# Storing the prompt's keys, values, gate scratch and mixer outputs through GpSimd's DMA queue

## The chip, the cores and the metric

The kernel runs on one core of a Trainium2 chip. The metric is the device time of one execution in microseconds. Three runs of the kernel before took 1498.4, 1499.0 and 1500.19 us, the median is 1499.0.

A core has five engines, each with an instruction queue of its own that runs strictly in order: TensorE (PE), VectorE (DVE), ScalarE (ACT), GpSimd (POOL) and SyncE (SP), which only issues transfers. A transfer (DMA) is issued from an engine's queue and then moved by the core's 16 DMA engines. Issuing stops the queue until the data that the transfer reads is ready and its target is free.

## The reference

One layer of a hybrid decoder, for a prompt of 2048 rows and 64 sample rows. What is computed:

```python
h = rms_norm(x, g_norm); proj = h @ w_in            # 1024 -> 3584
u, va, za, q, k, vb, zb = split(proj)
# mixer A: 4 groups of 128 channels, chunks of 128 rows
a = rms_norm(u * (tril(w_s) @ rms_norm(va) + b_s)) * silu(za)
# mixer B: 8 heads of 64; q, k normalised; patterns (128,1), (512,4), (2048,16)
for (w, r) in PATTERNS:                             # query t sees t - j*r, j = 0..w//r
    o_i, lse_i = banded_softmax_attention(q, k, vb, w // r, r)
b = rms_norm(sum_i softmax_i(lse) * o_i) * silu(zb)
h = x + concat(a, b) @ w_out
y = h + sigmoid(h @ w_ple_gate) * rms_norm(p @ w_ple)
# outputs: y (prompt, sample), k and vb of the prompt, k, vb and va of the samples
```

The sample rows do the same against a cache of 2048 keys and values for each of 8 sequences.

## The kernel before

The input projection is done in eight column chunks, `order = A0, B0, B1, A1, B2, B3, A2, A3`: A chunks hold u, v, z of one gMLP group, B chunks q, k, v, z of two heads (a head pair). Each chunk goes over 16 tiles of 128 prompt rows and one of the 64 sample rows (`gemm`, L441), three accumulators in PSUM. After every four tiles (512 rows) a group is finished:

- `b_norm` (L496 and on) normalises q and k and writes to HBM: the keys `ko` and values `vo`, which are outputs, the values in half-precision halves `v16` (to `vscr`, read back by the attention's `vload`), and the gate `gz` (to `zscr`).
- `a_norm` and later `a_mix` (L605 and on) compute the gMLP group, in place in the tile `ua`, and store it into `catd` (L634), 512 columns wide for mixer A.

Attention (`attn`, `scores`, `stage_c`) runs in small units that a pump in the program slips between the matmuls of the next chunks. Each unit takes scores, splits the exponentials into two halves `pc` on VectorE, lets SyncE transpose them by DMA into `pT` (L712), and multiplies with the values. Each pattern's partial result `rec` goes to HBM (r1d, r2d, r3d).

When a head pair is through, `comb_load` (L815, L818) loads the three partial results (`rl`, three buffers in all) and the gate (`gzl`, one buffer) for 512 rows, and `combine` merges them: the subtractions and `rl` merges (L826 to L835), a square, a reciprocal root on GpSimd (L187), the product with the gate (L850), and the store into `catd` (L852). Four combinations follow one another for each head pair. Those of the last pair (B3) run while chunk A3 is projected; at the same time the weights of the output stage are loaded (`wprep3`, L864), squared for their scale (L873), and split into halves (L888, L889), and the sample rows' attention begins, in which GpSimd multiplies cache rows with queries (L1184).

The output stage (`p3_*`) reads `catd` rows, tile by tile, and makes y.

The buffers that matter: `vo` and `ko` share two (`tmpA`), `gz` has two, `ua` two (`raw`), `gzl` one. A buffer is free again when its store has landed.

The order on each engine's queue is not the program's: the framework lists the instructions by a model of their times (`schedule_with_timeline_sim=True`), so an edit in one place can move instructions on all engines behind it.

Of the kernel before, what the change touches and what calls it, by code (L numbers as in the profile page):

```python
# [21 lines left out]
P = 128  # L22
# [119 lines left out]
def tile_hymba_gmlp_dilated_attn_step(  # L142
# [6 lines left out]
    nc = tc.nc  # L149
# [10 lines left out]
    kwin = k_win.rearrange("l b s h d -> (l b s) (h d)")  # L160
    vwin = v_win.rearrange("l b s h d -> (l b s) (h d)")
# [15 lines left out]
    def nm(s):  # L177
        uid[0] += 1
        return f"{s}_{uid[0]}"


    def small(n, tag=None, bufs=4, p=P):
        return sml.tile([P, n], F32, name=nm("sm"), tag=tag or f"s{n}", bufs=bufs)

    def rsqrt(src, n, p=P):
        y = small(n, f"rsy{n}")[:p]
        nc.gpsimd.tensor_tensor(y, src, mhalf[:p, :n], op=ALU.pow)  # L187
        return y
# [50 lines left out]
    zscr = [drm.tile([T, P], F32, name=f"zscr{i}") for i in range(4)]  # L239
# [3 lines left out]
    catd = [drm.tile([512, D], F32, name=f"catd{i}") for i in range(4)]  # L243
# [252 lines left out]
    def b_norm(G, sc, gch):  # L496
        m, n, hp, jg = G["m"], G["n"], G["hp"], G["jg"]
        c0 = hp * P
        ms = small(16, "bms", 2)
        nc.vector.tensor_scalar(ms[:m, :4 * n], G["ss"][:m, :4 * n], 2.0 ** -24 / HD, sc[:m, 5:6], op0=ALU.mult, op1=ALU.add)  # L500
        y = rsqrt(ms[:m, :4 * n], 4 * n, m)
        y4 = y.rearrange("p (j a) -> p j a", a=4)
        kv = G["raw"][:m, :n, 128:256].rearrange("p j (h d) -> p j h d", d=HD)
        qv = G["raw"][:m, :n, 0:128].rearrange("p j (h d) -> p j h d", d=HD)
        if m == P:
            ko = wk.tile([P, 4, P], F32, name=nm("ko"), tag="tmpA", bufs=2)
            for q in range(n):
                for h in range(2):
                    nc.vector.scalar_tensor_tensor(qv[:, q, h], qv[:, q, h], y4[:, q, h:h + 1], gqk,
                                                   op0=ALU.mult, op1=ALU.mult)  # L510
                nc.vector.tensor_tensor(kv[:, q], kv[:, q], y4[:, q, 2:4].unsqueeze(2).to_broadcast([P, 2, HD]),
                                        op=ALU.mult)
                nc.vector.tensor_tensor(ko[:, q, :].rearrange("p (h d) -> p h d", d=HD), kv[:, q],
                                        gkS.unsqueeze(1).to_broadcast([P, 2, HD]), op=ALU.mult)
        else:
            for h in range(2):
                nc.vector.scalar_tensor_tensor(qv[:, 0, h], qv[:, 0, h], y4[:, 0, h:h + 1], gqS[:m],
                                               op0=ALU.mult, op1=ALU.mult)
                nc.vector.scalar_tensor_tensor(kv[:, 0, h], kv[:, 0, h], y4[:, 0, h + 2:h + 3], gkS[:m],
                                               op0=ALU.mult, op1=ALU.mult)  # L520
        gzv = G["gz"][:m, :n, :]
        nc.vector.tensor_tensor(gzv, gzv, gch[:m, 0, :].unsqueeze(1).to_broadcast([m, n, P]), op=ALU.mult)
        if m == P:
            r0 = jg * 512
            rows = lambda t, a, w: t[r0:r0 + 512, a:a + w].rearrange("(j p) c -> p j c", p=P)
            nc.sync.dma_start(rows(kwin, c0, P), ko)
            nc.sync.dma_start(rows(vwin, c0, P), G["vo"])
            nc.sync.dma_start(rows(vscr[hp], 0, 258), G["v16"])
            nc.sync.dma_start(rows(zscr[hp], 0, P), G["gz"])
        else:  # L530
            gs = G["gz"][:m, 0, :]
            nc.vector.tensor_scalar(gs, gs, sc[:m, 2:3], None, op0=ALU.mult)
            qo, ko, vo = G["raw"][:m, 0, 0:128], G["raw"][:m, 0, 128:256], G["vo"][:m, 0, :]
            nc.sync.dma_start(knew[:, c0:c0 + P], ko)
            nc.sync.dma_start(kd[:, c0:c0 + P], ko)
            nc.sync.dma_start(vnew[:, c0:c0 + P], vo)
            nc.sync.dma_start(vd[:, c0:c0 + P], vo)
            nc.sync.dma_start(qd[:, c0:c0 + P], qo)
            nc.sync.dma_start(gzd[:, c0:c0 + P], gs)
# [65 lines left out]
    def a_mix(G, sc, gch):  # L605
        m, n, g, jg = G["m"], G["n"], G["g"], G["jg"]
        c0 = g * P
        pm = pst("t", 1)
        if m == P:
            with behind():  # L610
                nc.tensor.matmul(pm, lhsT=wsT[:, g, 0, :], rhs=G["vh"], start=True, stop=False)
            nc.tensor.matmul(pm, lhsT=wsT[:, g, 0, :], rhs=G["vl"], start=False, stop=False)
            nc.tensor.matmul(pm, lhsT=wsT[:, g, 1, :], rhs=G["vh"], start=False, stop=True)
            bb, mul = bsT, cS
        else:
            with behind():
                nc.tensor.matmul(pm[:m, 0:P], lhsT=bd8[:, g, :], rhs=G["va"][:m, 0, :], start=True, stop=True)
            bb, mul = bsS, 1.0
        pv = pm[:m, :n * P].rearrange("p (j c) -> p j c", c=P)
        t = G["va"][:m, :n, :]  # L620
        nc.vector.scalar_tensor_tensor(t, pv, mul, gch[:m, 1, :].unsqueeze(1).to_broadcast([m, n, P]),
                                       op0=ALU.mult, op1=ALU.mult)
        nc.vector.scalar_tensor_tensor(t, t, bb[:m, g:g + 1], G["u"][:m, :n, :], op0=ALU.add, op1=ALU.mult)
        s2 = small(4, "as2", 2)
        for q in range(n):
            nc.scalar.activation(G["u"][:m, q, :], t[:, q, :], AF.Square, accum_out=s2[:m, q:q + 1])
        ms = small(4, "ams", 2)
        nc.vector.tensor_scalar(ms[:m, :n], s2[:m, :n], 1.0 / P, sc[:m, 3:4], op0=ALU.mult, op1=ALU.add)
        y = rsqrt(ms[:m, :n], n, m)
        nc.vector.tensor_scalar(y, y, sc[:m, 2:3], None, op0=ALU.mult)  # L630
        for q in range(n):
            nc.vector.scalar_tensor_tensor(t[:, q], t[:, q], y[:, q:q + 1], G["gz"][:m, q, :], op0=ALU.mult, op1=ALU.mult)
        if m == P:
            nc.sync.dma_start(catd[jg][:, c0:c0 + P].rearrange("(j p) c -> p j c", p=P), t)  # L634
        else:
            nc.sync.dma_start(cats[:, c0:c0 + P], t[:, 0, :])

# [183 lines left out]
    def combine(hp, jg, sc, rr, gz):  # L821
        e = small(24, "e24", 2).rearrange("p (i a) -> p i a", i=3)
        nb = [t[:, :, HD + 1] for t in rr]
        mn = small(8, "mn8", 2)
        nc.vector.tensor_tensor(mn, nb[0], nb[1], op=ALU.min)
        nc.vector.tensor_tensor(mn, mn, nb[2], op=ALU.min)  # L826
        for i in range(3):
            nc.vector.tensor_tensor(e[:, i, :], mn, nb[i], op=ALU.subtract)
        ef = e.rearrange("p i a -> p (i a)")
        nc.scalar.activation(ef, ef, AF.Exp)  # L830
        t0 = rr[0][:, :, 0:65]
        nc.vector.tensor_tensor(t0, t0, e[:, 0, :].unsqueeze(2).to_broadcast([P, 8, 65]), op=ALU.mult)
        for i in (1, 2):
            for a in range(8):
                nc.vector.scalar_tensor_tensor(t0[:, a], rr[i][:, a, 0:65], e[:, i, a:a + 1], t0[:, a],  # L835
                                               op0=ALU.mult, op1=ALU.add)
        o = rr[0][:, :, 0:64]
        sq = rr[1][:, :, 0:64]
        nc.scalar.activation(sq, o, AF.Square)
        ss = small(8, "css", 2)  # L840
        nc.vector.tensor_reduce(ss, sq, axis=AX.X, op=ALU.add)
        dn = small(8, "cdn", 2)
        nc.vector.tensor_tensor(dn, rr[0][:, :, 64], rr[0][:, :, 64], op=ALU.mult)
        nc.vector.tensor_scalar(dn, dn, sc[:, 4:5], None, op0=ALU.mult)
        nc.vector.scalar_tensor_tensor(dn, ss, 1.0 / HD, dn, op0=ALU.mult, op1=ALU.add)
        y = rsqrt(dn, 8)
        nc.vector.tensor_scalar(y, y, sc[:, 2:3], None, op0=ALU.mult)
        g8 = gz.rearrange("p j (h d) -> p (j h) d", h=2)
        for a in range(8):
            nc.vector.scalar_tensor_tensor(g8[:, a], o[:, a], y[:, a:a + 1], g8[:, a], op0=ALU.mult, op1=ALU.mult)  # L850
        c0 = 512 + hp * P
        nc.sync.dma_start(catd[jg][:, c0:c0 + P].rearrange("(j p) c -> p j c", p=P), gz)  # L852

    big = {}

# [475 lines left out]
    for ci, (kind, i) in enumerate(order):  # L1331
# [9 lines left out]
        G = None  # L1341
        for j in range(NT + 1):
# [25 lines left out]
            if j % 4 == 0 and j < NT:  # L1368
                G = (b_group if kind == "B" else a_group)(i, j // 4, 4, P)
# [120 lines left out]
```

## Time and profile before

| | |
|---|---|
| median of 3 runs | 1499.0 us |
| profiled execution | 1500.87 us |
| its span | 1499.2 us |
| TensorE busy | 1299.3 us, 87% |
| VectorE busy | 1059.2 us, 71% |
| ScalarE busy | 781.1 us, 52% |
| GpSimd busy | 313.9 us, 21% |
| DMA, SyncE's queue | 262.73 MB, 78.7% of 16 engines |
| DMA, GpSimd's queue | 1.66 MB, 0.7% of 16 engines |
| granted TensorE clock | 0.95 of full |

Busy time is a share of the whole span; it says little about a single stage, where another engine or a transfer may come last. The stages by time: weights and A0 up to some 125 us, projection with attention up to some 880, the combination of the last head pair with the loads of the output weights up to some 1020, then the output stage with the sample rows' attention. The 80 stores that the change touches lie between 82.3 and 1016.1 us.

### The profile page before, as it was taken

To read this page: it belongs to the slowest core of one execution; us is meant where nothing else is said; L and a number is where in the kernel's file an instruction comes from. 1 tells how busy PE (TensorE), PEld (TensorE's weight loads), DVE (VectorE), ACT (ScalarE), POOL (GpSimd) and SP (SyncE) were. 2 spreads that over 40 slices of the span, in tenths; PEclk is the share of its full clock that TensorE was granted. 3 is DMA by queue.
4 is the path that set the end of the run, shared out by engine and by line. 5 is a ranking of instruction groups with operands and counts; after the bars stand their busy time and mean duration, and the time that the engine had idled before them with its cause. 6 is when DMAs were issued, how large, how long until landed. Compare 5 with 4: busy or idle time off the path is not lost.

```text
span 1499.2 us, 26289 instructions
## 1 busy us (share of the span) xinstructions
PE 1299.3 (87%) x8472; PEld 669.7 (45%) x8472; DVE 1059.2 (71%) x3659; ACT 781.1 (52%) x2163; POOL 313.9 (21%) x279
## 2 busy tenths in 40 slices
PE   2889997996889998896779887598989899989998
PEld 1444454553556444453446643353433343434443
DVE  4456786788888789787889787797556564555544
ACT  5666666775658755686565866545122222221222
POOL 8212001010210212110112034321331331430101
PEclk9999999996999999997889999799999999999999
DMA  6993688698976678967897599688799998996442
GB/s 169 234 202 98 126 172 171 145 182 170 215 145 133 146 172 174 198 144 178 181 205 153 130 239 255 195 213 175 185 236 250 209 239 193 209 263 130 107 95 64
DMA packets 591434, 266.06 MB, mean 177 GB/s; under 512 B 338336, under 2 KB 568800, under 8 KB 591296
## 3 DMA queue, kind: packets, MB, share of 16 engines
q1 hardware_dynamic: 589312, 262.73, 78.7%
q0 software_dynamic: 1984, 1.66, 0.7%
q8 instruction: 66, 1.08, 0.3%
q14 instruction: 72, 0.59, 0.1%
HBM read 134.56 MB, written 48.01 MB: 122 GB/s over the span
## 4 chain that ended last, share of the span: by engine, by line
PE 31%; DMA 26%; DVE 20%; ACT 10%; SPq 5%; issue 4%; POOL 3%; POOLq 0%; DVEq 0%; ACTq 0%
PE psg L441 10%; PE psg L932 8%; PE pss L932 7%; DMA pT<-pc 6%; DMA K<-in_cache_k_dram 4%; ACT sm L769 3%; DMA rl<-r3d 3%; DMA qB<-qd 2%; DVE sm L761 2%; DVE rl L835 2%; DMA qk<-qkc 2%; SPq L425 2%; POOL K L1184 2%; DVE pc L773 2%; PE pso L1264 2%
## 5 line engine op out<-in xcount | busy, mean ns | idle before, releaser
L441 PE MATMUL psg<-wt,xT 128*128 128x512 f16 (+1 forms) x3072 | 636.8, 363 | 36.5 <-DMA xT<-xhl 21.3
L441 PEld LDWEIGHTS <-xT 128*128 128x128 f16 x3072 | 302.1, 101 | 321.3 <-issue 52.4
L187 POOL TENSOR_TENSOR sm<-sm,mhalf 128x1 f32<-128x1 f32 (+5 forms) x115 | 150.6, 1313 | 784.3 <-DVE sm L500 335.6
L769 ACT ACTIVATE sm<-sm,rec,psc 128x256 f32<-128x256 f32 (+1 forms) x384 | 185.6, 548 | 63.1 <-DVE rec L765 61.5
L932 PEld LDWEIGHTS <-Th 128*128 128x128 f16 x800 | 76.9, 99 | 114.8 <-issue 26.0
L761 DVE CUSTOM_DVE_ANT_0 sm<-pss,mask 128x256 f32<-128x256 f32 (+1 forms) x384 | 122.6, 362 | 6.1 <-PE pss L755 2.0
L932 PEld LDWEIGHTS <-Tc 128*128 128x128 f16 x800 | 77.0, 98 | 104.4 <-issue 13.2
L1184 POOL TENSOR_TENSOR K<-K,qB 96x512 f32<-96x512 f32 x64 | 87.6, 1373 | 167.6 <-DMA qB<-qd 98.3
L773 DVE TENSOR_TENSOR pc<-sm,pc 128x512 f16<-128x512 f32 (+1 forms) x160 | 104.7, 655 | 1.6
L794 PEld LDWEIGHTS <-pT 128*128 128x128 f16 x600 | 58.0, 100 | 104.9 <-DMA pT<-pc 101.1
L1185 DVE TENSOR_REDUCE blk<-K 96x8 f32<-96x512 f32 x64 | 43.4, 680 | 81.3 <-POOL K L1184 81.3
L932 PE MATMUL psg<-w,Th 128*128 128x512 f16 x400 | 97.4, 386 | 3.8 <-DMA Th<-hl 3.8
L932 PE MATMUL pss<-w,Th 128*128 128x512 f16 x400 | 96.0, 383 | 0.0
L932 PE MATMUL psg<-w,Tc 128*128 128x512 f16 x400 | 93.8, 380 | 1.8 <-DMA Tc<-hl 1.7
L932 PE MATMUL pss<-w,Tc 128*128 128x512 f16 x400 | 94.3, 379 | 0.0
L919 ACT ACTIVATE hl<-x,sm 128x1024 f16<-128x1024 f32 (+1 forms) x17 | 19.5, 1147 | 140.6 <-DVE sm L900 112.0
L755 PEld LDWEIGHTS <-qk 128*128 128x128 f16 x960 | 76.0, 122 | 37.1 <-issue 12.2
L772 DVE CAST pc<-sm 128x512 f16<-128x512 f32 (+1 forms) x160 | 66.3, 415 | 34.8 <-ACT sm L769 33.1
L794 PE MATMUL pso<-vt,pT 128*128 128x65 f16 x352 | 43.7, 198 | 39.6 <-DMA pT<-pc 34.6
L1021 POOL TENSOR_TENSOR tg<-tg,x 128x1024 f32<-128x1024 f32 (+1 forms) x16 | 37.5, 2347 | 181.6 <-DVE tg L1020 169.6
L755 PE MATMUL pss<-kc,qk 128*128 128x128 f16 x704 | 61.7, 231 | 10.5 <-DVE sm L761 10.5
L794 PE MATMUL pso<-v,pT 128*128 128x65 f16 x248 | 33.6, 203 | 41.9 <-DMA pT<-pc 36.6
(314 smaller groups left out, 2271.5 us busy)
## 6 DMA issues: line engine op xcount, KB each, us to landing
qB<-qd SPq DMA_DIRECT2D x64, 192.0 KB
K<-in_cache_k_dram SPq DMA_DIRECT2D x64, 192.0 KB
V<-in_cache_v_dram SPq DMA_DIRECT2D x64, 192.0 KB
vt<-vscr SPq DMA_DIRECT2D x32, 258.0 KB
K<-in_cache_k_dram SPq DMA_DIRECT2D x32, 256.0 KB
V<-in_cache_v_dram SPq DMA_DIRECT2D x32, 256.0 KB
cat<-catd SPq DMA_DIRECT2D x16, 512.0 KB
x<-in_x_prompt_dram SPq DMA_DIRECT2D x16, 512.0 KB
```

Of the source, the lines that this page charges most:

```text
L187: nc.gpsimd.tensor_tensor(y, src, mhalf[:p, :n], op=ALU.pow)
L441: last_mm[0] = nc.tensor.matmul(g[:, :ncol], lhsT=l, rhs=r, start=(n == 0), stop=(n == (23 if j < NT else 15)))
L755: nc.tensor.matmul(pss[:, s, h, b * w:(b + 1) * w], lhsT=Q[:, h, qs], rhs=keys(h, k), start=(i == 0 and b == 0), stop=(i == 1 and b == n - 1))
L761: nc.vector.tensor_tensor_reduce(sm4[:, s, h], pss[:, s, h], mk, 1.0, -3.0e38, op0=ALU.add, op1=ALU.max, accum_out=mx[:, i:i + 1])
L769: nc.scalar.activation(sm4[:, s, h], sm4[:, s, h], AF.Exp, bias=r[:, sl + s, h, HD + 1:HD + 2], scale=psc)
L772: nc.vector.tensor_copy(pc[:, :n], smv)
L773: nc.vector.tensor_tensor(pc[:, n:2 * n], smv, pc[:, :n], op=ALU.subtract)
L794: nc.tensor.matmul(po[:, s, h, 0:65], lhsT=H, rhs=v[:, vs_, a:a + 65], start=(bi == 0), stop=False)
L932: last_mm[0] = nc.tensor.matmul(gs[hf], lhsT=o[part][:, kt], rhs=w[:, kt % 2, half, :], start=(n[hf] == 0), stop=(n[hf] == (3 if m == P el ...
L1021: (nc.vector if end else nc.gpsimd).tensor_tensor(t[:m, sl], t[:m, sl], s["x"][:m, sl], op=ALU.add)
L1184: nc.gpsimd.tensor_tensor(K3, K3, qB, op=ALU.mult)
L1185: nc.vector.tensor_reduce(s3[:, b, :, ts_].rearrange("p h t -> p t h"), K3.rearrange("p t (h d) -> p t h d", d=HD), axis=AX.X, op=ALU.add)
```

## The change

Five stores, each in a place that runs 16 times, are issued from GpSimd's queue in place of SyncE's. The store of `v16` stays on SyncE, and so do all loads, the transposes, and the sample rows' stores.

```diff
@@ b_norm
-            nc.sync.dma_start(rows(kwin, c0, P), ko)
-            nc.sync.dma_start(rows(vwin, c0, P), G["vo"])
+            nc.gpsimd.dma_start(rows(kwin, c0, P), ko)
+            nc.gpsimd.dma_start(rows(vwin, c0, P), G["vo"])
             nc.sync.dma_start(rows(vscr[hp], 0, 258), G["v16"])
-            nc.sync.dma_start(rows(zscr[hp], 0, P), G["gz"])
+            nc.gpsimd.dma_start(rows(zscr[hp], 0, P), G["gz"])
@@ a_mix
-            nc.sync.dma_start(catd[jg][:, c0:c0 + P].rearrange("(j p) c -> p j c", p=P), t)
+            nc.gpsimd.dma_start(catd[jg][:, c0:c0 + P].rearrange("(j p) c -> p j c", p=P), t)
@@ combine
-        nc.sync.dma_start(catd[jg][:, c0:c0 + P].rearrange("(j p) c -> p j c", p=P), gz)
+        nc.gpsimd.dma_start(catd[jg][:, c0:c0 + P].rearrange("(j p) c -> p j c", p=P), gz)
```

The order on the other engines moves with it, on TensorE from some 155 us on, on VectorE and ScalarE a little earlier. On SyncE, at the second combination of the last head pair (`rl_12662` is the third partial result for the third combination, `gzl_12664` its gate, `catd_118<-gzl_12468` the second combination's store, `w3st` are gate weights), before:

```order
L864 DMA w3st_13463<-in_w_ple_gate_dram 128x2x512
L864 DMA w3st_13507<-in_w_ple_gate_dram 128x2x512
L864 DMA w3st_13509<-in_w_ple_gate_dram 128x2x512
L864 DMA w3st_13511<-in_w_ple_gate_dram 128x2x512
L864 DMA w3st_13513<-in_w_ple_gate_dram 128x2x512
L815 DMA rl_12660<-r2d_112 128x4x132
L634 DMA catd_117<-ua_12593 128x4x128
L852 DMA catd_118<-gzl_12468 128x4x128
L815 DMA rl_12662<-r3d_116 128x4x132
L818 DMA gzl_12664<-zscr_104 128x4x128
L634 DMA catd_118<-ua_12929 128x4x128
```

The same place on SyncE after the change:

```order
L815 DMA rl_12660<-r2d_112 128x4x132
L1234 DMA V_2473_14087<-in_cache_v_dram 96x4x128
L1234 DMA V_2474_14089<-in_cache_v_dram 96x4x128
L1140 DMA V_13742<-in_cache_v_dram 128x4x128
L815 DMA rl_12662<-r3d_116 128x4x132
L818 DMA gzl_12664<-zscr_104 128x4x128
L864 DMA w3st_13461<-in_w_ple_gate_dram 128x2x512
L864 DMA w3st_13463<-in_w_ple_gate_dram 128x2x512
L864 DMA w3st_13507<-in_w_ple_gate_dram 128x2x512
```

The load of `rl_12662` no longer follows the store of the combination ahead, and all eight loads of gate weights have moved behind the load of `gzl_12664`.

On GpSimd, at the first combination of the last head pair (`K` are the multiplications for the sample rows, `sm_12371` is this combination's reciprocal root), before:

```order
L1184 TENSOR_TENSOR K_2198_12856<-K_2198_12856,qB_12858 96x512
L187 TENSOR_TENSOR sm_12371<-sm_12367,mhalf 128x8
L1184 TENSOR_TENSOR K_2226_12965<-K_2226_12965,qB_12967 96x512
L187 TENSOR_TENSOR sm_12888<-sm_12886,mhalf 64x1
L187 TENSOR_TENSOR sm_12921<-sm_12919,mhalf 128x4
L1184 TENSOR_TENSOR K_2228_12971<-K_2228_12971,qB_12973 96x512
L1184 TENSOR_TENSOR K_2245_13077<-K_2245_13077,qB_13079 96x512
```

The same place on GpSimd after the change:

```order
L1184 TENSOR_TENSOR K_2198_12856<-K_2198_12856,qB_12858 96x512
L634 DMA catd_120<-ua_12292 128x4x128
L1184 TENSOR_TENSOR K_2226_12965<-K_2226_12965,qB_12967 96x512
L187 TENSOR_TENSOR sm_12371<-sm_12367,mhalf 128x8
L187 TENSOR_TENSOR sm_12888<-sm_12886,mhalf 64x1
L187 TENSOR_TENSOR sm_12921<-sm_12919,mhalf 128x4
L1184 TENSOR_TENSOR K_2228_12971<-K_2228_12971,qB_12973 96x512
L852 DMA catd_117<-gzl_12275 128x4x128
L1184 TENSOR_TENSOR K_2245_13077<-K_2245_13077,qB_13079 96x512
```

Two stores now stand between the multiplications, and the reciprocal root comes one multiplication later.

## Rows read from the trace of the kernel before

**Rows 1.** The page: SyncE's DMA queue (packets, MB, share), the chain by engine.

```profile
q1 hardware_dynamic: 589312, 262.73, 78.7%
...
PE 31%; DMA 26%; DVE 20%; ACT 10%; SPq 5%; issue 4%; POOL 3%; POOLq 0%; DVEq 0%; ACTq 0%
```

**Rows 2.** Busy time by stretch: attention, full DMA engines, last combinations.

```profile
core 0: us, PE busy (x) PEld busy (x) DVE busy (x) ACT busy (x) POOL busy (x), PEclk, DMA share, GB/s
880.00:945.00 65.00, 51.88 (x270) 26.18 (x269) 50.32 (x146) 41.51 (x129) 31.95 (x25) 0.92 1.01 238
945.00:1017.00 72.00, 55.75 (x283) 28.15 (x282) 59.33 (x214) 36.39 (x121) 18.67 (x12) 0.88 0.76 207
155.00:820.00 665.00, 568.16 (x4558) 325.43 (x4557) 552.51 (x2353) 440.44 (x1265) 92.59 (x52) 0.93 0.80 167
```

**Rows 3.** SyncE's waits: us in total, times, longest.

```profile
SPq L712 <- DVE pc L773: 71.8, 57, 4.6
```

**Rows 4.** The page: GpSimd's DMA issues, KB each, median us to landing.

```profile
blk<-in_g_ple_dram POOLq DMA_DIRECT2D x1, 512.0 KB, 4.5
...
w<-in_w_s_dram POOLq DMA_DIRECT2D x1, 256.0 KB, 8.1
```

**Rows 5.** Timeline of GpSimd: start us, us; the 256 KB load.

```profile
4.22 0.76 POOL L290 DMA_DIRECT2D w<-in_w_s_dram  x1
```

**Rows 6.** Chain of waits at A0's first two stores: start us, us, what.

```profile
82.30 0.45 SPq L634
...
103.98 1.23 SPq L429
...
105.30 2.64 DMA catd<-ua
```

**Rows 7.** Timeline of VectorE: the second group's output.

```profile
100.59 1.14 DVE L632 SCALAR_TENSOR_TENSOR ua<-ua,sm,agz 128x128 f32<-128x128 f32 x4
```

**Rows 8.** Who waited for whom, whole span: us in total, times, longest.

```profile
PE pso L794 <- DMA pT<-pc: 71.2, 58, 3.6
...
DVE sm L826 <- DMA rl<-r3d: 20.2, 15, 3.2
...
ACT ua L576 <- DMA catd<-ua: 14.4, 4, 6.6
```

**Rows 9.** Chain of waits: one transpose, then the last head pair's combinations.

```profile
172.71 3.36 DMA pT<-pc
...
919.98 7.23 DMA rl<-r3d
...
956.18 0.73 ACT junk L873 x2
...
963.88 1.57 DVE gzl L850 x8
...
965.89 4.00 DMA rl<-r3d
...
982.20 3.08 DMA rl<-r3d
```

**Rows 10.** Timeline of SyncE: gate weights, the gate's load.

```profile
945.37 0.47 SPq L864 DMA_DIRECT2D w3st<-in_w_ple_gate_dram  x1
...
948.02 4.49 SPq L864 DMA_DIRECT2D w3st<-in_w_ple_gate_dram  x5
...
969.16 0.36 SPq L818 DMA_DIRECT2D gzl<-zscr  x1
...
976.08 0.46 SPq L864 DMA_DIRECT2D w3st<-in_w_ple_gate_dram  x1
```

**Rows 11.** Timelines of SyncE and ScalarE: the tightest store of values.

```profile
174.04 0.53 SPq L527 DMA_DIRECT2D out_dram<-vo  x1
...
176.75 0.37 ACT L491 ACTIVATE vo<-psg,sm 128x128 f32<-128x128 f32 x1 [1.47 <-DMA out_dram<-vo]
```

**Rows 12.** The page's groups: the cast of the probabilities.

```profile
L772 DVE CAST pc<-sm 128x512 f16<-128x512 f32 (+1 forms) x160 | 66.3, 415 | 34.8 <-ACT sm L769 33.1
```

## The prediction

> **What bounds the kernel now.** I read the chain of waits on the page first, then the table by stretches, then who waits for whom, and last the timelines around the stores. The chain spreads over everything: TensorE 31%, DMA 26%, VectorE 20%, and only 5% is SyncE's own issuing [rows 1]. So there is no single wall. The stretches say more [rows 2]. While attention runs (155 to 820 us) TensorE is busy 568 of 665 us, VectorE 553, and the 16 DMA engines 0.80 of the time. From 880 to 945 us the DMA engines are full (share 1.01). From 945 to 1017 us, where the last head pair is combined and the output stage begins, nothing is full: TensorE is busy 56 of 72 us, VectorE 59. That last stretch is where waits, not work, set the pace.
>
> Next: does SyncE's queue hold anything up? Most of the time it does not: before the transposes of the probabilities (L712) it already stands idle until VectorE has written the halves, 57 times for 71.8 us in all [rows 3]. Taking 80 issues of about 0.4 us from a queue that is waiting anyway gives back nothing by itself. It matters only where a store stands in the queue, itself not ready or behind transposes, with something urgent behind it.
>
> **The change, part by part.** The sum is made against the profiled execution, 1500.9 us, of which 1499.2 is the span; that is 1.9 above the median of 1499.0, so I carry the sum over to the median. 80 stores leave SyncE's queue (16 each of ko, vo, gz, and of the two mixers' outputs). Each takes 256 KB in 512-byte rows. GpSimd has one DMA of just that size and row length in the trace, a load: it held GpSimd for 0.76 us [rows 5] and landed after 8.1 us, at the crowded start; its 512 KB load landed after 4.5 us [rows 4]. On SyncE the same store landed in 2.64 us [rows 6]. So a landing through GpSimd lies between 2.64 and 8.1 us; I take 4.5, the row that lies between them, 1.9 more than now.
>
> *First: the first gMLP group's outputs.* The store at 82.30 stands on the chain with 0.45 us of SyncE time, 0.5 with its gaps [rows 6]; it goes. The next group's output was finished by VectorE at 101.73 (100.59 + 1.14) [rows 7], but its store was issued at 105.30, behind the transposes of x (one more, 1.23 us, just ahead), and landed at 107.94, for which ScalarE waited [rows 6, 8]. GpSimd is free at 101.73: with 4.5 the store lands at 106.2, 1.7 earlier; with 2.64 it is 3.6 earlier, with 8.1 it is 1.9 later. Term: -2.2 (from -4.1 to +1.4).
>
> *Second: the combination of the last head pair.* In the order of before, the load of the third partial result for the next combination stands behind the store of this one, which waits for its last instruction (L850). The chain goes through just that three times: loads of 7.23, 4.00 and 3.08 us, 14.3 together, each begun right after the store [rows 9]. In the new order that load stands free of it, and its buffer is released earlier, at the last L835. What is late next is VectorE, busy 82% of that stretch [rows 2], and the gate rows' load. I take half: -7 (from -14.3 to 0). The same unblocking for the other head pairs is part of the 20.2 us that VectorE waits for these loads [rows 8]; VectorE there has other work right behind, so I count it at nothing.
>
> *Third: buffers released later.* Values: at 174.04 the store of vo was issued and ScalarE waited for it until 176.75, 1.47 us [rows 11]. That is the tightest of the sixteen. 1.9 us more of landing and about 1 us behind the reciprocal root on GpSimd make 2.8; three accumulators of the projection wait in PSUM meanwhile, so half: +1.5 (0 to +9: there 8.1 - 2.7 = 5.4 in full, and two thirds of that again over the other fifteen). gMLP outputs of the later groups: three of ScalarE's four waits for them, 14.4 - 6.6 = 7.8 us, were behind no queue [rows 8]; at 1.9 each they grow by 5.7, half on the path: +3 (0 to +8, half of three times 5.5).
>
> *Fourth: GpSimd's time.* 80 x 0.76 = 61 us more, beside 93 us of work in the 665 us of attention [rows 2]: idle time covers it. Uncovered it would be 0.76 before a root that VectorE waits for, some ten times: 0, bounds 0 and +8. The new order shows the one place where a store stands ahead of other work that is urgent: the two stores between GpSimd's multiplications for the decode keys, around 915 us, where the DMA engines are full and the multiplications wait for their loads anyhow.
>
> Sum: -2.2 - 7 + 1.5 + 3 + 0 = -4.7. On the profiled execution 1496.2, on the median's scale 1494.
>
> The Trainium skill speaks against the change here (SBUF — State Buffer, section SBUF: two separate sides): while VectorE runs a copy or cast in its two-port mode, GpSimd cannot write descriptors, and its DMA looks blocked. The trace has 160 casts that may be of that kind, of 415 ns [rows 12]; no DMA of GpSimd's runs beside one of them in a row shown here, so the lock is not seen yet. By the rule, if every store met one, landings would come 0.4 us later, a fifth more than my 1.9, and the sum would be -3.8 in place of -4.7.
>
> **Rivals.** *A, hidden (1499).* The combination is paced by VectorE and by loads of weights, not by the third partial result; the new waits are hidden as well. For it: VectorE's 82%, and that ScalarE and SyncE both had other causes of delay there. Against it: three visits of the chain to the same load.
>
> *B, slower: the gate weights behind the gz load.* In the new order SyncE's load of gz for the third combination (L818) stands ahead of all eight gate-weight loads (L864), and it waits until GpSimd's store of the second combination has landed, since gz has one buffer. Today six of those loads go out from 945.37 to 952.5 and the last at 976.08, the gz load at 969.16 [rows 10]. If the second combination ends when it does now (L850 done at 965.5 [rows 9]), gz can load at 965.5 + 4.5 = 970, the eight loads, 0.9 us each, go out until 977, 1 us later than now; but of the 16 squares of 0.73 us [rows 9] twelve, which now run before, come after them: 8.8 us. Price about +10, and the second term is lost: 1499 + 2.3 + 10 = 1511. It decides if the second combination's store lands after about 960. Against it: that combination was held up by those very squares in ScalarE, and the new order puts them behind it.
>
> *C, slower: transposes share the engines with the stores.* Today a store and the transposes lie in one queue, which holds 78.7% of the engines' time [rows 1]; a transpose issued ahead of a store is not touched by it. On a second queue a store would take turns with transposes already under way. Price: 64 stores in attention (48 and 16), each making one transpose later by half its 2.64 us: 84 us of latency; TensorE's waits for these transposes are 71.2 us [rows 8] of 160 x 3.36 = 538 us of latency [rows 9], 13%, so +11: with my sum 1499 - 4.7 + 11 = 1505. Against it: today the transposes behind a store wait for all of it, so what some lose others gain. The Trainium skill has the rule (DMA: Bandwidth & Descriptors, section SWDGE vs HWDGE vs iDMA): the two kinds of issue feed different queues inside each DMA engine, which takes them in turn. By it C happens to some extent; no run yet shows how much.
>
> *D, all of the second term comes (1486)*, -14.3 in place of -7, if VectorE's waits fill with later work.
>
> **How the numbers follow.** A measurement of this kernel tells 0.2% from no change, 3 us. Forecast 1494: 0.40; D: 0.08; A: 0.18; B: 0.19; C: 0.15. The forecast's own spread, 1488 to 1500, puts 0.04 of its 0.40 within 3 us, and 0.01 of C lies there too. So faster 0.36 + 0.08 = 0.44, same 0.18 + 0.05 = 0.23, slower 0.19 + 0.14 = 0.33. The order of all engines is made anew, which adds a spread that no row prices; the range, 1482 to 1512, takes in D and B.
>
> **What would show it.** Right: in the profile after, the load of the third partial result starts before L850 of the combination ahead of it, and the waits of VectorE for it are well under 20 us; the stretch from 945 to the output stage is shorter by 5 to 8 us; ScalarE's waits for the stores of ua and vo grow by less than 10 us. Wrong: GpSimd's stores land after more than 6 us (third term), SyncE's L818 waits more than 10 us more in all with the gate weights late (B), or TensorE waits clearly longer than 71 us for the transposes (C). If SyncE's shorter queue alone moved the time, my first reading, that it waits for VectorE anyway, is wrong.

## The result and the profile after: slower by 0.8%

The changed kernel takes 1512.98 us (median of four, 1509.09 to 1513.52) against 1499.6 of the kernel before on the same chip (four runs, 1498.4 to 1500.63). The ratio is 1.0078, 95% interval 1.0054 to 1.0102: 13 us slower, where 5 us faster were forecast. The profiled execution took 1509.09 us and is the fastest of the four, so it shows some 8 of the 13 us.

From its page (engines: busy us, share; then packets; then queue, packets, MB, share of 16 DMA engines):

```profile
PE 1305.5 (87%) x8472; PEld 672.0 (45%) x8472; DVE 1061.8 (70%) x3659; ACT 780.7 (52%) x2163; POOL 375.9 (25%) x359
...
DMA packets 555594, 266.06 MB, mean 177 GB/s; under 512 B 338336, under 2 KB 527840, under 8 KB 555456
...
q1 hardware_dynamic: 547072, 241.75, 73.0%
q0 software_dynamic: 8384, 22.64, 5.4%
```

The bytes moved as intended: 20.98 MB from SyncE's queue (q1) to GpSimd's (q0) [rows 1]. GpSimd is busy 62 us longer, as the fourth step said. But the same stores are cut otherwise: on SyncE's queue they were 42,240 packets, 528 for each store; on GpSimd's they are 6,400, 80 for each. TensorE, which does the same work, is busy 6 us longer: it had the higher clock for a smaller part of the span, 0.944 against 0.95.

How the stores landed, from the same page (KB each, median us from issue to landing):

```profile
catd<-ua POOLq DMA_DIRECT2D x16, 256.0 KB, 4.4
out_dram<-vo POOLq DMA_DIRECT2D x16, 256.0 KB, 4.0
zscr<-gz POOLq DMA_DIRECT2D x16, 256.0 KB, 4.0
out_dram<-ko POOLq DMA_DIRECT2D x16, 256.0 KB, 3.8
catd<-gzl POOLq DMA_DIRECT2D x16, 256.0 KB, 3.8
```

That is a little better than the 4.5 us I took. Who waited for whom after (us in total, times, longest):

```profile
PE pso L794 <- DMA pT<-pc: 81.1, 58, 4.2
...
DVE sm L826 <- DMA rl<-r3d: 16.7, 11, 4.3
...
ACT ua L576 <- DMA catd<-ua: 12.4, 5, 5.3
```

ScalarE's waits for stores did not grow [rows 8]; its wait for vo [rows 11] is gone. What grew is TensorE's wait for the transposed probabilities, from 71.2 to 81.1 us. But these two profiles can't show the cause: of the 7.9 us between their spans 6.2 are TensorE's busy time at the lower clock, and its idle time in all only went from 199.9 to 201.6 us, since other waits are shorter in the new order (TensorE's for x's transposes 10.2 us, where they were 21.3). A place where a late transpose can be seen, in the timelines of SyncE, GpSimd and TensorE and in the chain of waits (start us, us, what):

```profile
547.55 1.23 SPq L712 DMA_TRANSPOSE pT<-pc  x1
```
```profile
547.58 0.79 POOL L529 DMA_DIRECT2D zscr<-gz  x1
```
```profile
554.15 0.24 PE L794 MATMUL pso<-v,pT 128*128 128x65 f16 x1 [4.08 <-DMA pT<-pc]
```
```profile
547.55 6.55 DMA pT<-pc
```

SyncE issues a transpose, GpSimd issues a store 0.03 us later, and the transpose is through after 6.55 us, where one took 3.36 before [rows 9]. TensorE stands for 4.08 us meanwhile. It looks like rival C, but the place alone doesn't show it: two weight loads had gone out just ahead on SyncE's queue (first line), and the chain of before, too, has a transpose of 6.00 us (second line):

```profile
545.52 0.98 SPq L342 DMA_DIRECT2D wst<-in_w_in_dram  x2
```
```profile
414.36 6.00 DMA pT<-pc
```

And an edit here also gives every engine a new order, so the first question was which of the two costs the time.

### The profile page after: what moved, and what is told of

Its sections match the earlier page's. It is cut to its first block, busy times and chain, and to the rows that moved or that the text cites. A ratio compares the mean times of both kernels' runs of the same rounds, so it can differ in the third digit from the quotient of the medians.

```text
span 1507.1 us, 26354 instructions
## 1 busy us (share of the span) xinstructions
PE 1305.5 (87%) x8472; PEld 672.0 (45%) x8472; DVE 1061.8 (70%) x3659; ACT 780.7 (52%) x2163; POOL 375.9 (25%) x359
## 4 chain that ended last, share of the span: by engine, by line
PE 38%; DMA 24%; DVE 18%; ACT 9%; issue 4%; SPq 4%; POOL 2%; ACTq 0%; DVEq 0%; POOLq 0%
PE psg L441 12%; PE psg L932 10%; PE pss L932 9%; DMA pT<-pc 6%; ACT sm L769 3%; DMA K<-in_cache_k_dram 2%; DMA qB<-qd 2%; DVE rl L835 2%; DMA rl<-r3d 2%; DVE sm L761 2%; DMA wst<-in_w_in_dram 2%; DVE pc L773 2%; PE pso L1264 2%; DMA rl<-r2d 2%; DMA qk<-qkc 2%
## 5 line engine op out<-in xcount | busy, mean ns | idle before, releaser
L772 DVE CAST pc<-sm 128x512 f16<-128x512 f32 (+1 forms) x160 | 66.6, 417 | 36.1 <-ACT sm L769 35.8
```

The lines of the kernel that those rows point to most:

```text
L772: nc.vector.tensor_copy(pc[:, :n], smv)
```

## The experiments

Each was timed against the kernel before on its own chip, whose median was 1507.9 us for the first four on record (the two that part queue and order, ScalarE's queue, and keys, values and gates), 1507.0 for the copies and the first mixers, 1506.5 for GpSimd's operations, the missing stores and the mixers alone, and 1496.7 for the last. So ratios are compared, not times; the times in the expectations are meant for a chip on which the kernel before takes 1499 us.

### Queue or order

Two kernels separate them. The program is traced twice: the first trace, with one set of queues, gives the order in which the scheduler issues everything; in the second, with the other set, this order is pinned on all five engines, and only the 80 stores are placed anew.

```diff
+    nc = build(THIS, issued(build(ORDER_OF)))
...
+    for engine in PINNED:                       # all five
+        row = [n for n in order[engine] if n in traced]
+        for a, b in zip(row, row[1:]):
+            tc.add_manual_dep(traced[b], a, info, reason="order")
```

*New queue, old order.*

> The changed kernel's five stores on GpSimd's queue, but every engine issues everything else in exactly the order of the kernel before (the program is traced twice and the first trace's order is pinned on the second). Theory ORDER: the stores themselves cost little and the 13 us of the change come from the new issue order that the scheduler made; then this run loses them: 1490 to 1502 us. Theory QUEUE: the 80 stores on GpSimd's queue (their packets beside the transposes', or GpSimd's time) cost the 13 us; then this run still has them: 1508 to 1516 us. By the sum of the prediction it would be near 1494.

Measured: 1.0097 (1.0062 to 1.0132), +15 us; its eight executions lie widely apart, from 1512.2 to 1529.42 us. The granted clock is not the reason: on the mean it is 0.945 here and 0.944 for the kernel before on that chip. *Old queue, new order:*

> The converse: the five stores stay on SyncE's queue as before, and every engine issues everything else in the order of the changed kernel. Theory ORDER: 1508 to 1518 us, the loss with no store moved. Theory QUEUE: 1496 to 1503 us.

Measured: 1.0024 (1.0001 to 1.0048), +4 us. The queue costs most of it; the theory ORDER falls but for a small part. The two don't add up: 0.78 less 0.24 leaves 0.54%, 8 us, for the queue in the new order, as the difference of two ratios, against 0.97% in the old one.

*The same five stores on ScalarE's hardware queue, old order* (one of them is shown):

```diff
-            nc.gpsimd.dma_start(rows(kwin, c0, P), ko)
+            nc.scalar.dma_start(rows(kwin, c0, P), ko)
...
```

> The five stores are issued on ScalarE's hardware queue, all else in the order of the kernel before. It takes them off SyncE's list too, without GpSimd's software queue. Theory QUEUE with the software queue's descriptors or GpSimd as the cause: back to about 1500 (1495 to 1504). Theory QUEUE with the cause that the stores now run beside the transposes instead of in line with them: as slow as the changed kernel, 1508 to 1516. Theory ORDER: about 1495 to 1504, unless a store that waits at the head of ScalarE's list holds up its activations, which would show as waits of ScalarE for the stores' tiles and add 5 to 20 us.

Measured: 1.0022 (1.0001 to 1.0043), +3 us. A second queue beside the transposes is not what costs 15 us; GpSimd's queue is. On balance the move to ScalarE gains nothing either. What a shorter SyncE queue gives by itself this run doesn't tell, for SyncE now stands at the load of the gate (L818, one buffer) until the attention mixer's store on the other queue has landed. SyncE's waits there, before, with the new queue in the old order, and with ScalarE's queue (us in total, times, longest):

```profile
SPq L818 <- DMA catd<-gzl: 9.2, 10, 2.7
```
```profile
SPq L818 <- DMA catd<-gzl: 29.0, 11, 5.3
```
```profile
SPq L818 <- DMA catd<-gzl: 30.0, 12, 5.2
```

They are as long on either queue, so they aren't what makes GpSimd's the dearer one.

*Parts of the change, old order:* first the stores of keys, values and gates alone.

> Only the stores of keys, values and gates (48 of the 80) on GpSimd's queue, the mixers' 32 stay on SyncE's, all else in the order of the kernel before. Theory ORDER: 1495 to 1503. Theory QUEUE: 48/80 of 13 us, so 1505 to 1510. By the prediction's terms the mixers' stores carried the gain (-2.2 and -7), so this one would be at 1500 to 1505.

Measured: 1.0052 (1.003 to 1.0074). And the mixers' stores alone:

> Only the mixers' 32 stores on GpSimd's queue, keys, values and gates stay on SyncE's, all else in the order of the kernel before. All 80 cost +0.97% and the other 48 +0.52%, so +0.3 to +0.6% (+5 to +9 us) if the costs add up. By the prediction's terms these 32 carry its gains (-2.2 at the first chunk, -7 at the last combinations): -9 to 0 us.

Measured: 1.0024 (1.0007 to 1.0042). Every part costs, and 0.52 + 0.24 = 0.76 lies within the interval of the whole. The 32 stores that were to carry the gain carry a loss.

### GpSimd's time, or the transposes

```diff
+            work(nc, cst, mhalf, "ko", ko)      # beside each store, which stays on SyncE:
+        nc.gpsimd.tensor_tensor(junk[kind], t[:, 0, 0:2], mhalf[:, 0:2], op=ALU.pow)
```

> Stores and order of the kernel before, and beside each of the 80 stores one GpSimd operation of about 0.8 us on two columns of the store's tile, whose result nobody reads. It puts GpSimd's 61 us of extra time at the places of the change, without a store on its queue. Theory GPSIMD TIME (its own list is longer, the reciprocal roots behind it come later): +6 to +15 us over the kernel before on the same chip. Theory DMA ENGINES (the transposes are late because the stores' packets run beside them): 0 to +3 us.

Measured: 0.9995 (0.9979 to 1.0012), with GpSimd busy 383.3 us, 69 more than before. GpSimd's time costs nothing that can be measured, and neither does pinning the order, which this run does too.

This kernel and the one with the new queue in the old order issue the same work in the same order, so their traces can be laid side by side (they come from two chips, on which the kernel before takes 1506.5 and 1507.9 us; the granted clocks are 0.943 and 0.944). The issue of the transposes on SyncE (shortest, median and longest issue in ns, first and last start in us), and TensorE's and ScalarE's waits, first with the stores on SyncE (and the idle operations on GpSimd), then on GpSimd:

```profile
L712 SPq DMA_TRANSPOSE pT<-pc x160: 1188/1236/2498, 160.8 to 880.2; - x160
```
```profile
PE pso L794 <- DMA pT<-pc: 74.4, 57, 4.3
...
ACT ua L576 <- DMA catd<-ua: 13.0, 4, 4.8
...
ACT vo L491 <- DMA out_dram<-vo: 1.5, 1, 1.5
```
```profile
L712 SPq DMA_TRANSPOSE pT<-pc x160: 1188/1247/2902, 160.5 to 903.9; - x160
```
```profile
PE pso L794 <- DMA pT<-pc: 92.1, 62, 3.7
...
ACT ua L576 <- DMA catd<-ua: 18.9, 5, 6.8
...
ACT vo L491 <- DMA out_dram<-vo: 6.1, 3, 2.6
```

From the first transpose to the last 719.4 us pass in the one and 743.4 in the other: 24.0 us, which is all of the difference between these two profiled executions (1504.41 and 1528.41). The output stage gives and takes nothing. TensorE's idle time (span less busy time) grew by 22.8 us, and its waits for the transposes are 17.7 of them. The second execution is near the slowest of its eight, so the price stays the 15 us of the ratio. With the stores on ScalarE's queue, in the same order, the waits for the transposes hardly grew:

```profile
PE pso L794 <- DMA pT<-pc: 76.8, 60, 4.5
```

One transpose, the same in both, with a store on GpSimd just ahead of it (timelines of GpSimd, SyncE and TensorE):

```profile
171.92 0.80 POOL L527 DMA_DIRECT2D out_dram<-vo  x1
```
```profile
171.94 1.24 SPq L712 DMA_TRANSPOSE pT<-pc  x1
```
```profile
177.35 0.23 PE L794 MATMUL pso<-v,pT 128*128 128x65 f16 x1 [3.62 <-DMA pT<-pc]
```

and with that store on SyncE, behind the transpose:

```profile
172.11 1.23 SPq L712 DMA_TRANSPOSE pT<-pc  x1
```
```profile
175.79 0.20 PE L794 MATMUL pso<-v,pT 128*128 128x65 f16 x1 [1.74 <-DMA pT<-pc]
```

5.4 us from issue to the matmul against 3.7. Over all transposes that TensorE's weight loads waited for (more than 0.15 us) in both traces, the time from SyncE's issue to the end of that wait, and how much later it is than with the stores on SyncE:

| stores on | a store issued within 3 us of the transpose | none |
|---|---|---|
| GpSimd's queue | +1.00 us (23 transposes, 23 us in all) | +0.16 us (37) |
| ScalarE's queue | +0.36 us (25) | +0.13 us (39) |

So the transposes that meet a store on GpSimd's queue are late, the others hardly, and on ScalarE's queue the delay is a third. The standard errors of 1.00 and 0.36 are 0.23 and 0.17, so the two queues differ by some two standard errors.

### Bytes and packets

64 of the stores were made a second time, to a scratch tensor, on another queue, old order, all real stores on SyncE.

```diff
+        copies[0](nc)(d.rearrange("(j p) c -> p j c", j=4), t)    # GpSimd or ScalarE
+        copies[0](nc)(d.rearrange("(p j) c -> p j c", j=4), t)    # third run: ScalarE, 2,048-byte rows
```

> Order and stores of the kernel before, and 64 of its stores (keys, values, gates, attention mixers) are made a second time, to a scratch tensor that nobody reads, on GpSimd's queue: 512-byte rows in memory, as the real ones. If a store on the software queue delays the transposes, and that is where the time goes, 64 of them cost what 64 of the 80 moved ones did: +9 to +15 us over the kernel before on the same chip. If the moved stores cost by being released late or by their place alone, +0 to +5 us.

> The same 64 extra stores on ScalarE's hardware queue, 512-byte rows. Theory SOFTWARE QUEUE (its 4,096-byte packets or the way it is served delay the transposes more than another hardware queue does): clearly less than on GpSimd's queue, +2 to +7 us. Theory ANY SECOND QUEUE (what runs beside the transposes delays them, whatever the queue): as much as on GpSimd's, +9 to +15 us.

> The same 64 extra stores on ScalarE's hardware queue, but to 2,048-byte rows in memory, so that its packets are four times as long and a quarter as many. Theory LONG PACKETS (a transpose's 256-byte packets wait behind long ones): 4 us or more above the run with 512-byte rows, near that on GpSimd's queue. Theory SOFTWARE QUEUE ITSELF, or bytes alone: the same as with 512-byte rows within 2 us.

Measured: 1.0243 (1.0209 to 1.0276), 1.0202 (1.017 to 1.0235) and 1.021 (1.0178 to 1.0243). All three expectations were far too low: an added store costs 0.5 us on ScalarE's queue, and all 64 bring 16.8 MB on top and hold their buffers for two landings. As a price for a moved store the runs are no use. They say two things. GpSimd's queue is the dearer one again, by 6 us at the median (1545.72 and 1539.87), though the intervals overlap. And on ScalarE's queue long packets cost no more than short ones at the median (1540.03), but with six executions each, a difference of 4 us, as the theory LONG PACKETS wants, isn't ruled out.

*Without the stores of keys and values:*

> The 32 stores of keys and values are left out altogether (those two outputs are not written), all else in the queue and order of the kernel before. It shows what 32 stores cost on SyncE's queue, and so the most that taking them off it could give. By the 64 extra stores on ScalarE's queue, which cost 33 us (0.5 us each), leaving 32 out gives -10 to -18 us: then a store costs what its bytes cost, on whichever queue, and moving it can give little. If stores in line on SyncE's queue cost nothing (the transposes would wait for their data anyway): -3 to +1 us.

Measured: 0.9963 (0.9946 to 0.998), -5.6 us, 0.17 us for each store, so between the two expectations. That is all that taking these 32 off SyncE's queue could give, if they cost nothing elsewhere; how much of it is the queue and how much the bytes, the run doesn't tell.

### Versions

*Only the first chunk's mixers on GpSimd:*

```diff
-            nc.sync.dma_start(catd[jg]..., t)
+            (nc.gpsimd.dma_start if g == 0 else nc.sync.dma_start)(catd[jg]..., t)
```

> Only the first chunk's four mixer stores on GpSimd's queue (before any transpose of the attention), all else in the queue and order of the kernel before. By the chain of waits these four gain what the prediction's first term said, and nothing pays for it: -2 to -3 us (ratio 0.998 to 0.9987). If even they cost time by delaying the loads and transposes of that stage: 0 to +2 us.

Measured: 0.9988 (0.9965 to 1.0011): the size is as expected, but not told from no change. *With fewer packets on SyncE's queue besides* (the store of the gates is shown; their load, and store and load of r1d, are changed alike):

```diff
-            nc.sync.dma_start(rows(zscr[hp], 0, P), G["gz"])
+            nc.sync.dma_start(zscr[hp][r0:r0 + 512].rearrange("(p j) c -> p j c", j=4), G["gz"])
...
```

> A version that the experiments point to, in the order of the kernel before: nothing but the first chunk's four mixer stores goes to GpSimd's queue, and the gates' scratch and the first pattern's result, which this kernel alone writes and reads, lie in memory with each partition's four rows behind one another, so that 64 of SyncE's transfers move in packets of 2,048 and 2,112 bytes (88 and 86 ns in the trace of before) and not four times as many of 512 and 528 (27 and 28 ns). That takes about 0.2 us of each DMA engine's time per transfer, 12 us in all. If transfers cost the kernel by the engine time that they take from the transposes: with the first mixers' -2 us, -4 to -8 us (ratio 0.995 to 0.997). If only bytes count, as the extra stores with long and with short rows suggest (2.10% and 2.02%): -2 us, as the first mixers alone.

Measured: 1490.68 us against 1496.73, ratio 0.9969 (0.995 to 0.9988): faster than the kernel before, and so than the changed one. Its page and its waits:

```profile
DMA packets 565066, 266.06 MB, mean 179 GB/s; under 512 B 338336, under 2 KB 533984, under 8 KB 564928
```
```profile
PE pso L794 <- DMA pT<-pc: 66.3, 56, 3.9
```

26,368 packets fewer for the same bytes, and TensorE's waits for the transposes below those of before (71.2 [rows 8], in one execution each). How much is the packets' and how much the first mixers', these two runs don't settle.

## Why the prediction was wrong, step by step

The forecast was 1494 us (1482 to 1512), measured were 1513. Two steps of the sum failed: the second term, and the transposes, for which it carried nothing.

*First term, the first gMLP stores (-2.2): right at its place.* After the change the second group's store runs at once, in the chain of waits:

```profile
99.18 0.40 DVE ua L632 x2
99.71 0.36 DVE ua L632
...
100.61 4.39 DMA catd<-ua
```

It lands at 105.0, 2.9 us earlier than before [rows 6]. In the time of the whole kernel the gain of these stores was not told from nothing (0.9988).

*Second term, the last head pair's combination (-7): the step that failed first.* I wrote that the load of the third partial result would stand free of the store ahead, its buffer released "at the last L835". The first half came true, the second did not. The chain of waits after, at two combinations, and SyncE's timeline (its lines have SPq):

```profile
946.82 2.13 DVE rl L835 x3
...
958.31 1.67 DVE gzl L850 x8
959.99 3.02 DMA rl<-r3d
...
993.02 1.45 DVE gzl L850 x7
...
995.59 3.52 DMA rl<-r3d
```
```profile
949.32 0.43 SPq L815 DMA_DIRECT2D rl<-r1d  x1
...
994.33 1.17 SPq L920 DMA_TRANSPOSE Tp<-hl  x1
```

The load still begins only when L850 has ended, with no store ahead of it: 0.01 us after it at the first place, 1.1 us after it at the second, where a transpose of the output stage stood ahead on SyncE (until 995.50). The three buffers are handed on as they come free. The first load gets the one that the last L835 releases (948.95, the load at 949.32), and the third gets the last, the first partial result's, which L850 reads to its end. The store had only stood behind the same event: before, the load began 0.44 us after L850's end (963.88 + 1.57 = 965.45, then 965.89) [rows 9], now 0.01. And the largest of the three visits, 7.23 us, was no wait for L850, which had ended at 917.31 (915.74 + 1.57), 2.7 us before that load was issued: it was a long transfer in the stretch in which the DMA engines were full (1.01 [rows 2]). The sign I named, a load that starts before L850, did not appear. From the last transpose (877.3 before, 887.9 after) to the end pass 621.9 and 619.2 us: 3 us gained where 7 were forecast, and in the old order none.

*Third term (+4.5): the landing was sized right,* 3.8 to 4.4 us for 4.5, but not what it is compared with: the four stores on SyncE's queue that ScalarE waited for before took 2.4 to 4.6 us from issue to the end of that wait, 2.64 was one of them. In the order that the changed kernel has, the waits of ScalarE did not grow; in the old order they did, by 5.9 us for ua and 4.6 for vo between the two traces laid side by side.

*Fourth term (0): right,* by the run with GpSimd's operations alone. The lock on descriptor writes that I weighed from the Trainium skill (SBUF — State Buffer, SBUF: two separate sides) does not show in the trace after: of the 80 issues none took more than 0.86 us, and the 25 with such a cast (L772) beside them, up to 0.6 us after their end, landed after 3.8 us (median), the other 55 after 4.1.

*Rival B: no.* SyncE's waits of L818 for the store went from 9.2 to 13.1 us in the changed kernel, not by 10:

```profile
SPq L818 <- DMA catd<-gzl: 13.1, 8, 3.4
```

In the old order they did grow, to 29.0 and 30.0 us, but there ScalarE's queue cost 3 us in all.

*Rival C: this is what happened, through GpSimd's queue.* The sum had nothing for it. Its chance, 0.15, was too low; its price was not. I set +11 us for 64 stores; the side-by-side traces have 23 us of later transposes and 17.7 us more of TensorE's waits for them in one execution, and the median of that kernel is 15 us up. But C's reason, a second queue that takes turns with SyncE's, would hold for ScalarE's queue as well, where the waits grew by 2.4 us. I argued against it that a transpose behind a store on SyncE's queue waits for all of it today, so that some would gain what others lose. ScalarE's queue, where the balance is +3 us, nearly bears that out; GpSimd's queue does not. The Trainium skill's rule (DMA: Bandwidth & Descriptors, SWDGE vs HWDGE vs iDMA), that the two kinds of queue take turns in each DMA engine, agrees with the late transposes: +1.00 us beside GpSimd's stores, +0.16 without one. Without the second term and with C's +11 the sum is -2.2 + 4.5 + 11 = +13.3, 1512; that this meets the 1513 measured is in part chance, since the third term was 0 and the new order cost 4.

*The first reading was not refuted:* nothing shows SyncE's queue in the way. With the stores on ScalarE's queue it is as short, and nothing was gained on balance; without 32 of the stores, bytes and all, 5.6 us were.

**What stays open:** why a store on GpSimd's queue delays a transpose by 1.0 us and one on ScalarE's by 0.36. The packets differ (below), but 2,048-byte packets on ScalarE's queue cost no more than 512-byte ones at the median, and no run changed the packets of GpSimd's queue. Part of the 15 us may also be the later release of ua and vo: ScalarE's waits for them grew by 10.5 us, while TensorE's idle time other than for the transposes grew by 5.1. The share of each was not separated. And why the queue costs less in the new order, 8 us, was not looked into.

## What to carry to other kernels

Before a store is moved off a busy queue, look at what runs on the DMA engines at that moment, not at the queue: here a store beside a transfer that TensorE waits for made it late, 1.0 us through GpSimd's queue and 0.36 through ScalarE's. A chain that goes "last instruction, store, load" doesn't say that the load waited for the store; find out what frees the load's buffer. And where a scheduler makes the order anew with every edit, pin the old order on the new queues and the new order on the old ones: the two runs tell an edit's own cost from that of the reshuffle.

## What the runs showed of the hardware

- One and the same 256 KB store with 512-byte rows is 528 packets on a hardware queue and 80 on GpSimd's software queue. In the trace's records of packets, 5,504 packets of 4,096 bytes stand on GpSimd's queue after (median 179 ns each) and 384 before; those of 512 bytes on SyncE's queue take 27 ns.
- A store issued on GpSimd's queue held GpSimd for 0.75 to 0.86 us, and landed after 3.8 to 4.4 us (medians by kind), where on SyncE's queue, before, one took 2.64 [rows 6] and the four that ScalarE waited for 2.4 to 4.6.
- 80 GpSimd operations more (69 us) changed nothing that could be measured, 0.9995.
- The 24 us between the two traces in one order all lie in the stretch with the transposes, and the engines' work is the same: TensorE's busy time is 1305.6 and 1306.5 us. What was lost is waiting.
